# Modulation loads queued behind the written stores, and three fills written before the recurrence's preparation

## The chip, the cores and the metric

The kernel runs on one core of one Trainium2 chip. The metric is the device time of one execution in microseconds (us); lower is better. PE is the matrix engine, DVE the vector engine, ACT the scalar engine, POOL GpSimd and SP the sync engine. SP, ACT and POOL also issue transfers, each in the order of its own instruction stream.

## The reference, cut to what matters

The reference is two layers over 512 latent tokens of width 1024 with 256 context tokens. Each layer starts with a modulation: `silu(c) @ mod_w[i] + mod_b[i]` gives a shift, a scale and a gate.

```python
shift, scale, gate = jnp.split(s_lat @ mod_w[i] + mod_b[i], 3, axis=-1)
h = rms_norm(x, g_pre[i]) * (1.0 + scale[:, None]) + shift[:, None]
...
r, k, v, za, bg, cg, xb, zb = jnp.split(h @ w_in, EVEN_SPLITS, axis=-1)
ya, _, _ = rwkv_seq(rwkv_prep(h, r, k, v, *rw), S_f, S_b, r_k, lnx_w, lnx_b, True)
yb = bg * dwconv(cg * xb, sc_w, seg_len)
y = jnp.concatenate([ya * silu(za), yb * silu(zb)], axis=-1) @ w_out
```

The even layer projects the tokens to r, k, v and five more streams of width 1024. It runs a recurrence over the context in both directions, and then over the latents from the context's last states (`S_f`, `S_b`). The odd layer is a convolution module. The modulation matrix of both layers is 1024 x 3072.

## The kernel before, in words

**Pairs and projections.** The 16 heads are handled as 8 pairs of 128 channels. A projection is one 1024 x 128 column block of the weights. Its matmuls are done three times over 8 row blocks (a high part and a low part of each operand, without low by low), 24 matmuls into one PSUM bank. `project(p, which, rc, between)` does r, k or v (which = 0, 1, 2) of pair p: a context projection (named `pck`, `pcv`) if `rc` is given, then a call of `between`, then a latent projection (`plr`, `plk`, `plv`). The ACT and two DVE instructions of `shifted` (L437, L438, L440) mix neighbouring tokens into the result (`kc`, `vc`, `lk`, `lv`, `lr`) and so empty the bank. The latent result is stored to memory (`psp`) from POOL, L458. `gate(p, 24, "za")` is a projection `pza` with ACT (L874) and DVE (L875), stored from POOL too. k0 stands below for k of pair 0, za4 for the gate of pair 4.

**Weights.** `load_w` brings a block in two halves of 256 KB by SP into two raw buffers (`wrk`, `wrv`, ...). ACT casts each half (L129, `whk`, ...) and DVE subtracts (L130, `wlk`, ...); three buffers each hold the high and the low halves. SP can issue the next half when the subtraction has freed a raw buffer.

**Banks.** Projections alternate between two PSUM banks (`mm0`, `mm1`), so a projection waits until the result before the last one has been emptied. The recurrence's preparation uses the two banks of the tag `at`.

**The modulation in groups.** What the second part of the modulation needs is computed in 16 groups of 1 MB, four transfers of 256 KB and four matmul pairs each, called group 0 to group 15 here. `rest()` is called 17 times between other work. Call n computes group n - 1 and starts the loads of group n + 1. Even groups go to one set of buffers (`mwbtanhl`, `mwbxal`, from group 8 on `ectx`), odd groups to another (`mwr`). Groups 0 and 1 are loaded by SP (L974), the others by POOL (L976). Calls 0 to 3 follow k0, k1, v0 and v1 in `prep_ctx(0, rest)`; calls 4 to 7 stand in `lora` after its row blocks 1, 3, 5 and 7; the others follow in the preparation of pairs 2 and 3.

**The recurrence.** Context stages s = 0 to 3 take two pairs each (`chain_ctx`), latent stages s = 4 to 11 one pair each (`chain_lat`). While stage s runs, the stage after the next is prepared: `light` builds factors on DVE and ACT, `heavy` multiplies them, `solve` inverts a triangle (a chain of small DVE instructions L739 and L741), `merge` puts halves together. Within `heavy`, `pa` is four groups of matmuls (`pal`); each uses both `at` banks, and DVE empties them into `E` (L682). Fills are projections that only later stages need: `fills(x)` writes those that `FILL_R` and `FILL_Z` list under x. `fills(3)` is r3, za4, za5, za6, za7.

**What sets the order.** A scheduler lays out each engine's instruction stream at build time from the dependencies; among what is ready it takes first what was written first, except that the weights' casts go ahead as high priority. The engines then run these streams in order. `tc.issue_after(x)` puts what its block writes on x's engine behind x in that engine's stream, without a wait for x's end. The letters of a stage give the order in which the work is written; the middle entry is used for s = 2 and 3.

```python
STAGE = ("KLSMVHvF", "OPLSMHF", "OSPLMHFC")
...
for gi, (z, g) in enumerate(PA_ORDER if lat else ((0, 0), (1, 0))):
    with anchored(an, ha[gi if lat else 2 * gi]):
```

L is light, S solve, M merge, H heavy, F fills. After stage 3 the convolution branch of pair 0 (`conv_branch(0)`: `pcg`, `pxb`, `pbg`, `pzb`) is written, and then the latent stages.

Of the kernel before, what the change touches and what calls it, by code (L numbers as in the profile page):

```python
# [31 lines left out]
CONV_AFTER = (0, 2, 7, 6)  # L32
PA_ORDER = ((0, 1), (1, 0), (1, 1), (0, 0))
HEAVY = ("ANB", "ANBV")
STAGE = ("KLSMVHvF", "OPLSMHF", "OSPLMHFC")
FILL_R = (0, 0, 2, 3, 4, 4, 4, 4)
FILL_Z = (0, 1, 1, 1, 3, 3, 3, 3)
ZR = (slice(0, 64), slice(64, 128))
# [13 lines left out]
def kernel(ctx: ExitStack, tc: tile.TileContext, I: dict, out: bass.AP):  # L52
# [325 lines left out]
    def lora(hp, w1, between):  # L378
        pwl, pal = (ps.tile([P, 512], F32, tag="zo", name=n, bufs=2) for n in ("pwl", "pal"))
        pwc = ps_at("pwc")  # L380
        for kt in range(KT):
            h1 = hp[kt][:, 1:771]
            dh = w("AR", f"dh{kt}")[:, 0:770]
            V.tensor_tensor(out=dh, in0=hp[kt][:, 0:770], in1=hp[kt][:, 2:772], op=ALU.add)
            for (zi, pl) in ((0, pwl), (1, pal)):
                xw = E1[:, (2 * kt + zi) % 4 * D : (2 * kt + zi) % 4 * D + 770]
                S.activation(xw, h1, AF.Copy, scale=owa[:, zi * 8 + kt : zi * 8 + kt + 1])
                V.scalar_tensor_tensor(out=xw, in0=dh, scalar=hwa[:, zi * 8 + kt : zi * 8 + kt + 1], in1=xw,
                                       op0=ALU.mult, op1=ALU.add)
                lhs = w1[zi][kt // 4][:, kt % 4].rearrange("p a b -> p (a b)")  # L390
                mm(pl, lhs, xw[:, 258:770], kt == 0, kt == KT - 1)
                mm(pwc[:, zi * CTX : (zi + 1) * CTX], lhs, xw[:, 0:CTX], kt == 0 and zi == 0, kt == KT - 1 and zi == 1)
            if kt % 2:
                between()
        lorl.extend([cvp.tile([P, SEQ], F32R, tag=f"{t}{z}", name=f"{t}{z}") for z in range(2)] for t in ("tanhl", "xal"))
        S.activation(lorc[0], pwc[:, 0:CTX], AF.Tanh)
        S.copy(lorc[1], pwc[:, CTX : 2 * CTX])
        for i, pl in enumerate((pwl, pal)):
            t, th = w("tmp", f"lor{i}"), w("tmp", f"lorh{i}", F32R)
            S.activation(t, pl, AF.Copy if i else AF.Tanh)  # L400
            S.copy(th, t)
            for z in range(2):
                rows, hr, lr = (slice(64 * x, 64 * x + 64) for x in (z, i, 1 - i))
                S.copy(lorl[i][z][hr], th[rows])
                V.tensor_tensor(out=lorl[i][z][lr], in0=t[rows], in1=th[rows], op=ALU.subtract)
# [37 lines left out]
    def project(p, which, rc=None, between=None):  # L443
        nm = "rkv"[which] + str(p)
        wt = first_w.pop(nm) if nm in first_w else load_w(which * 8 + p, nm)
        if rc is not None:
            pc = (ps_at if nm in ("k0", "k1") else ps_mm)("pc" + nm)[:, :CTX]
            proj(wt, pc, (hch, hcl))
            shifted(pc, rc, p, which)
            if between:  # L450
                between()
        pl = ps_mm("pl" + nm)
        proj(wt, pl, hlat)
        flip["at"] ^= 1
        tag = ("cg", "yb")[flip["at"]]
        rl = cvp.tile([P, SEQ], F32, tag=tag, name="l" + nm)
        shifted(pl, rl, p, which)
        nc.gpsimd.dma_start(psp[p, which], rl)  # L458

    def state(lat, x):  # L460
        ps_ = [x] if lat else [2 * x, 2 * x + 1]
# [4 lines left out]
    def prep_ctx(b, between=None, st=None, kinds=(1, 2), inner=None, js=(0, 1)):  # L466
        st = st or state(False, b)
        for which in kinds:
            nm = "rkv"[which]
            if nm not in st:  # L470
                st[nm] = w("r_" if which == 1 and b % 2 else nm + "_", nm + st["nm"])
            for p, cs in [st["parts"][j] for j in js]:
                project(p, which, st[nm][:, cs], inner)
                if between:
                    between()
        return st
# [185 lines left out]
    def heavy(st, an=None):  # L662
        ha = (None,) * 4 if an is None else HEAVY_AFTER[an["lat"]]
        lat, nm = st["lat"], st["nm"]
        UV = buf("UV", st)
        E = buf("E", st)
        st["UV"], st["E"], st["BKt"] = UV, E, [buf("BKt", st, z) for z in range(2)]

        def pa():
            for gi, (z, g) in enumerate(PA_ORDER if lat else ((0, 0), (1, 0))):  # L670
                with anchored(an, ha[gi if lat else 2 * gi]):
                    AR, BK = st["AR"][z], st["BK"][z]
                    m, x = (4, P) if lat else (8, CH)
                    c0 = m * g
                    pas = [ch3(ps_at(f"pa{nm}{z}{g}{h}"), x) for h in range(2)]
                    go = pinned(st["ev"] if lat else ())
                    st["ev"] = []
                    for c in range(m):
                        for h in (1, 0):
                            go(pas[h][:, c, :], kb(BK, h, c0 + c), AR[ZR[h], c0 + c, 0:x])  # L680
                    for h in range(2):
                        st["ev"].append(V.tensor_tensor(  # L682
                            out=E[:, h, z * NLAT + c0 : z * NLAT + c0 + m, :], in0=pas[h],
                            in1=maskE[:, z * (1 + h) : z * (1 + h) + 1, 0:x].to_broadcast([P, m, x]), op=ALU.mult))

        def pb():
            for z in range(2):
                pbs = [ch3(ps_at(f"pb{nm}{z}{h}")) for h in range(2)]
                go = pinned(st["ev"] if lat else ())
                st["ev"] = []  # L690
                for c in range(NLAT):
                    for h in (1, 0):
                        go(pbs[h][:, c, :], kb(st["BK"][z], h, c), ident[ZR[h], ZR[h]], op=tr)
                for h in range(2):
                    st["ev"].append(S.copy(st["BKt"][z][:, :, ZR[h]], pbs[h]))

        def nt():
            for h in range(2):
                for b in range(2):
                    rs = slice(64 * (1 - h) + 32 * b, 64 * (1 - h) + 32 * b + 32)  # L700
                    S.copy(Nt[rs], E[rs, h, :, 32 * b : 32 * b + 32])

        def pv():
            pv, v_ = ch3(ps_at(f"pv{nm}")), st["v"]
            for c in range(NLAT):
                for h in range(2):
                    mm(pv[ZR[h], c, :], v_[ZR[h], c * CH : (c + 1) * CH], ctr[ZR[h], ZR[h]], True, True)
            for z in range(2):
                for h in range(2):
                    src = pv[ZR[h]].rearrange("p (j c) x -> p j c x", j=2)  # L710
                    dst = UV[ZR[h], z * NLAT : (z + 1) * NLAT, ZR[h]].rearrange("p (j c) x -> p j c x", j=2)
                    S.copy(dst, src if lat or not z else src[:, :, ::-1, :])

        def po():
            if lat:
                bon = st["bon"]
                pb = ps_at("pbon" + nm)
                mm(pb, blk, bon, True, True)
                V.scalar_tensor_tensor(out=bon, in0=pb, scalar=0.5, in1=st["v"], op0=ALU.mult, op1=ALU.mult)

        st["po"], st["pv"] = po, pv
        for x in HEAVY[lat]:
            {"A": pa, "B": pb, "N": nt, "V": pv, "O": po}[x]()
# [181 lines left out]
    def after(anchor):  # L905
        return tc.issue_after(anchor) if anchor is not None else nullcontext()
# [43 lines left out]
    def rest():  # L950
# [16 lines left out]
        for g in ((n + 1,) if n else (0, 1)):  # L967
            for q in ((0, 1, 2, 3), (3, 2, 1, 0))[g % 2] if g < 16 else ():
                u = 4 * (g // 8) + q
                layer, c0 = (0, 2 * D + 512 * u) if u < 2 else (1, 512 * (u - 2))  # L970
                src = I["mod_w"][layer, g % 8 * P : (g % 8 + 1) * P, c0 : c0 + 512]
                if g < 2:
                    with tc.issue_after(env["last"].ins):
                        nc.sync.dma_start(home(g, q), src)  # L974
                else:
                    nc.gpsimd.dma_start(home(g, q), src)  # L976

    def rested(half_, acc):
        row = w("HP", f"mrow{half_}")
# [10 lines left out]
        if half_ == 0:  # L990
            V.memset(acc, 0.0)

    def fills(x):
        for p in range(8):
            if FILL_R[p] == x:
                project(p, 0)
            if FILL_Z[p] == x:
                gz = gate(p, 24, "za")
                nc.gpsimd.dma_start(psp[p, 3], gz)

    sts = [prep_ctx(0, rest)]
    whs, behind = first_w["spectra"]
    with tc.issue_after(behind):
        for ns, wh in whs:
# [19 lines left out]
    for s in range(12):  # L1024
# [11 lines left out]
        for x in STAGE[(s >= 2) + (s >= 4)]:  # L1036
# [16 lines left out]
                light(sts[s + 2], st)  # L1053
            elif x == "H" and s < 10:
                heavy(sts[s + 2], st)
            elif x == "F":
                fills(s + 1)
                if s >= 4:
                    finish(st)
            elif x == "C":  # L1060
# [383 lines left out]
```

## Time and profile before

| | |
|---|---|
| median of 3 runs | 1385.95 us (1385.75 to 1392.3) |
| the profiled execution | 1392.7 us |
| its span, first to last instruction | 1390.9 us |
| busy: PE, DVE, ACT, POOL | 1337.1, 985.3, 745.3, 127.4 us |
| mean granted clock of PE | 0.992 |

A timeline row gives start and duration in us, the engine, the line, the operation, out<-in, and in brackets the engine's idle time before it and what ended that. A window row gives start and end, the length, the busy time and count of each engine (PE, weight loads, DVE, ACT, POOL), PE's granted clock (1 is full speed), the busy share of the DMA engines and GB/s.

### The profile page before, as it was taken

The numbers are of one execution on the slowest core, as the hardware profiler recorded it, in microseconds if no ns is written. First come the engines' busy times: TensorE is split into PE (matmuls) and PEld (weight loads), VectorE is DVE, ScalarE is ACT, GpSimd is POOL, SyncE is SP. The second block draws the span as 40 slices with busy tenths as digits, with TensorE's granted clock in tenths as the row PEclk, the third lists the DMA queues.
The fourth block names the chain that finished last, engine by engine and source line by source line (L and its number), as shares of the span: only waits on it lengthen the run. The fifth ranks groups of instructions, "written<-read, shape, count | busy, mean of one in ns | idle before, by whom it ended". The sixth has DMA issues, their size and how long they took to land.

```text
span 1390.9 us, 29758 instructions
## 1 busy us (share of the span) xinstructions
PE 1337.1 (96%) x11925; PEld 995.2 (72%) x11925; DVE 985.3 (71%) x2304; ACT 745.3 (54%) x1509; POOL 127.4 (9%) x263
## 2 busy tenths in 40 slices
PE   6989999999899999999999999999999999999998
PEld 2646777777677766676666676677777787788886
DVE  5846879868999599989999998557654653644323
ACT  6536366546756566665666755547742432554222
POOL 4123200001111010101101000010000000000000
PEclk9999999999999999999999999999999999999999
DMA  9855521222323312223222221578621322133232
GB/s 333 254 190 190 189 77 57 87 79 86 88 90 101 99 63 79 70 65 88 82 73 70 76 70 57 183 238 290 222 62 61 121 64 58 61 112 101 91 103 79
DMA packets 139756, 158.55 MB, mean 114 GB/s; under 512 B 15504, under 2 KB 104224, under 8 KB 139498
## 3 DMA queue, kind: packets, MB, share of 16 engines
q1 hardware_dynamic: 123152, 106.47, 24.7%
q0 software_dynamic: 15856, 49.12, 10.8%
q8 instruction: 94, 1.54, 0.5%
q10 hardware_dynamic: 608, 1.06, 0.2%
q14 instruction: 46, 0.37, 0.1%
HBM read 138.33 MB, written 18.28 MB: 113 GB/s over the span
## 4 chain that ended last, share of the span: by engine, by line
PE 66%; DVE 16%; ACT 6%; issue 6%; DMA 5%; SPq 0%; POOL 0%; DVEq 0%; ACTq 0%; POOLq 0%
PE pu L57 10%; PE pz L57 6%; PE f L57 6%; PE uh L57 4%; PE zol L57 4%; PE pcg L57 4%; PE o L57 4%; PE plk L57 3%; PE pxb L57 3%; PE plr L57 2%; PE plv L57 2%; PE pzb L57 2%; DVE E L682 2%; PE pck L57 1%; PE zoc L57 1%
## 5 line engine op out<-in xcount | busy, mean ns | idle before, releaser
L57 PE MATMUL o<-wh,y 128*128 128x512 f32 x248 | 79.7, 397 | 0.0
L739 DVE TENSOR_TENSOR xtmpl<-Xl,Yl 128x126 f32<-128x126 f32 (+22 forms) x248 | 61.9, 250 | 2.8
L741 DVE TENSOR_TENSOR Yl<-Yl,xtmpl 128x126 f32<-128x126 f32 (+22 forms) x248 | 61.9, 250 | 2.7
L1257 ACT CAST ah<-a 64x512 fp32r<-64x512 f32 x32 | 19.8, 618 | 72.6 <-DVE a L1252 72.2
L57 PE MATMUL zol<-UV,E 64*64 64x64 f32 (+1 forms) x1024 | 54.0, 221 | 0.0
L57 PEld LDWEIGHTS o<-wh,y 128*128 128x128 f32 x248 | 45.9, 188 | 9.5
L57 PE MATMUL o<-wl,y 128*128 128x512 f32 x124 | 49.6, 400 | 2.0 <-DVE wl L130 2.0
L57 PE MATMUL pal<-ARl,BKl 64*128 64x128 f32 x512 | 45.7, 298 | 5.8 <-DVE E L682 5.2
L57 PE MATMUL zol<-Hl,ARl 64*64 64x64 f32 x896 | 50.2, 230 | 0.7 <-DVE Hl L854 0.4
L847 ACT COPY UV<-uh 64x128 f32<-64x128 f32 x128 | 33.3, 260 | 32.5 <-PE uh L57 25.0
L57 PEld LDWEIGHTS zol<-Hl,ARl 64*64 64x64 f32 x896 | 34.9, 133 | 20.0 <-issue 15.1
L130 DVE TENSOR_TENSOR wl<-wr,wh 128x1024 fp32r<-128x1024 f32 x28 | 34.2, 1223 | 20.6 <-ACT wh L129 20.5
L57 PEld LDWEIGHTS pal<-ARl,BKl 64*128 64x128 f32 x512 | 36.1, 193 | 16.9 <-issue 10.2
L57 PEld LDWEIGHTS uh<-UV,BKt 128*64 128x64 f32 x704 | 26.3, 137 | 30.3 <-ACT UV L847 23.4
L1252 DVE TENSOR_TENSOR a<-pu,a 128x512 f32<-128x512 f32 x16 | 11.0, 690 | 47.7 <-PE pu L57 45.4
L57 PEld LDWEIGHTS zol<-UV,E 64*64 64x64 f32 (+1 forms) x1024 | 42.2, 136 | 2.8 <-ACT UV L847 2.1
L682 DVE TENSOR_TENSOR E<-pal,maskE 128x512 f32<-128x512 f32 x64 | 43.0, 682 | 0.5 <-PE pal L57 0.3
L1209 DVE SCALAR_TENSOR_TENSOR pr<-px,dbe,What 119x512 f32<-119x512 f32 x32 | 22.6, 747 | 26.6 <-PE px L57 26.6
L129 ACT CAST wh<-wr 128x1024 fp32r<-128x1024 f32 x28 | 29.6, 1057 | 21.3 <-PE o L57 10.7
L854 DVE SCALAR_TENSOR_TENSOR Hl<-uh,PCl,HPl 128x64 f32<-128x64 f32 x112 | 26.4, 277 | 19.4 <-PE uh L57 9.2
L57 PE MATMUL uh<-UV,BKt 128*64 128x64 f32 x704 | 36.3, 232 | 3.3 <-ACT UV L847 2.0
L57 PEld LDWEIGHTS uh<-Ol,E 64*64 64x64 f32 x512 | 19.9, 133 | 24.5 <-ACT Ol L841 17.3
(996 smaller groups left out, 4206.1 us busy)
## 6 DMA issues: line engine op xcount, KB each, us to landing
wr<-in_ev_w_out_dram SPq DMA_DIRECT2D x28, 512.0 KB, 5.2
mwr<-in_mod_w_dram POOLq DMA_DIRECT2D x28, 256.0 KB, 4.3
wrv<-in_ev_w_in_dram SPq DMA_DIRECT2D x16, 256.0 KB, 3.1
ectx<-in_mod_w_dram POOLq DMA_DIRECT2D x16, 256.0 KB, 4.2
wrr<-in_ev_w_in_dram SPq DMA_DIRECT2D x16, 256.0 KB, 2.9
wrza<-in_ev_w_in_dram SPq DMA_DIRECT2D x16, 256.0 KB, 2.8
wrcg<-in_ev_w_in_dram SPq DMA_DIRECT2D x16, 256.0 KB, 2.8
wrxb<-in_ev_w_in_dram SPq DMA_DIRECT2D x16, 256.0 KB, 3.0
```

The costliest lines, as they stand in the source:

```text
L57: env["pe"] = T.matmul(o, lhsT, rhs, start=start, stop=stop)
L129: S.copy(hi, raw)
L130: env["lo"].tensor_tensor(out=lo, in0=raw, in1=hi, op=ALU.subtract)
L682: st["ev"].append(V.tensor_tensor(out=E[:, h, z * NLAT + c0 : z * NLAT + c0 + m, :], in0=pas[h], in1=maskE[:, z * (1 + h) : z * (1 + h) + ...
L739: V.tensor_tensor(out=tv, in0=X[:, :i, i : i + 1].to_broadcast([P, i, m]), in1=Y[:, i : i + 1, c0:].to_broadcast([P, i, m]), op=ALU.mult)
L741: V.tensor_tensor(out=Y[:, :i, c0:], in0=Y[:, :i, c0:], in1=tv, op=ALU.add)
L847: u_ = S.copy(UV[ZR[1 - h], i : 2 * nch - i : 2 * nch - 1 - 2 * i, ZR[h]], uh[ZR[1 - h], 0:2, :])
L854: h_ = V.scalar_tensor_tensor(out=Hn[:, z, :], in0=uh[:, 2 + z, :], scalar=PC[z][:, i : i + 1], in1=HP[:, z, :], op0=ALU.mult, op1=ALU.add)
L1209: V.scalar_tensor_tensor(out=pr[s][:NPROD], in0=px[s][:NPROD], scalar=dbe[:, 0:1], in1=What[:, n * 512 : n * 512 + 512], op0=ALU.add, op1= ...
L1252: V.tensor_tensor(out=a, in0=pp[1], in1=a, op=ALU.mult)
L1257: S.copy(ahl[s][hr], a[hr])
```

## The change

There are two parts.

1. The POOL loads of a modulation group are put behind the last store of a latent r, k or v result that was written before them (`env["store"]`), in POOL's stream. One call of `rest()` is moved: it leaves `lora`'s row block 1 and stands inside v1, between its context and its latent projection. So group 2 is computed and group 4's load written inside v1 (before: after v1), group 3 is computed and group 5's load written after v1 (before: in `lora`'s row block 1); from call 5 on the calls stand where they stood.
2. In stage s = 2 three of the five fills (r3, za4, za5) are written ahead of `heavy` (letter f), the other two (za6, za7) after it as before. The last matmul of za5 is kept as `hold`, and the groups 1 to 3 of `pa` in that `heavy` are put behind it in PE's stream. Stage 3 has the letter too, but does nothing there.

```diff
-STAGE = ("KLSMVHvF", "OPLSMHF", "OSPLMHFC")
+STAGE = ("KLSMVHvF", "OPLSMfHF", "OSPLMHFC")
...
-            if kt % 2:
+            if kt % 2 and kt > 1:
                 between()
...
-        nc.gpsimd.dma_start(psp[p, which], rl)
+        env["store"] = nc.gpsimd.dma_start(psp[p, which], rl)
...
-                project(p, which, st[nm][:, cs], inner)
+                project(p, which, st[nm][:, cs], inner if b or (p, which) == (1, 2) else None)
...
-                with anchored(an, ha[gi if lat else 2 * gi]):
+                with anchored(an, ha[gi if lat else 2 * gi]), after(st.get("hold") if gi else None):
...
-                    nc.gpsimd.dma_start(home(g, q), src)
+                    with tc.issue_after(env["store"].ins):
+                        nc.gpsimd.dma_start(home(g, q), src)
...
-    def fills(x):
-        for p in range(8):
-            if FILL_R[p] == x:
+    def fills(x, first=0, last=None):
+        for kind, p in [(kind, p) for p in range(8) for kind in "RZ" if (FILL_R, FILL_Z)[kind == "Z"][p] == x][first:last]:
+            if kind == "R":
                 project(p, 0)
-            if FILL_Z[p] == x:
+            else:
...
-    sts = [prep_ctx(0, rest)]
+    sts = [prep_ctx(0, rest, inner=rest)]
...
+            elif x == "f" and s == 2:
+                fills(s + 1, 0, 3)
+                sts[s + 2]["hold"] = env["pe"].ins
             elif x == "F":
-                fills(s + 1)
+                fills(s + 1, 3 if s == 2 else 0)
```

## The prediction

> **What bounds the kernel now.** I read the page's busy shares and chain first, then the matrix engine's timeline for its idle times, and for each large one the timelines of the engines it waited for.
>
> ```profile
> PE 1337.1 (96%) x11925; PEld 995.2 (72%) x11925; DVE 985.3 (71%) x2304; ACT 745.3 (54%) x1509; POOL 127.4 (9%) x263
> PE 66%; DVE 16%; ACT 6%; issue 6%; DMA 5%; SPq 0%; POOL 0%; DVEq 0%; ACTq 0%; POOLq 0%
> ```
>
> PE is busy 1337.1 of 1390.9 us, so 53.8 us of idle time are all that reordering can win, and the change alters no arithmetic. The two largest idle times of PE after the first 10 us are these, each in a place that the change touches.
>
> ```profile
> 72.24 1.04 PE L57 MATMUL uh<-mwr,s 128*2 128x512 f32 x8
> 74.30 0.48 PE L57 MATMUL pcv<-hctx,whv 128*128 128x256 f32 x2 [1.02 <-DVE vc L440]
> 80.94 0.76 PE L57 MATMUL plv<-hlh,whv 128*128 128x512 f32 x1 [3.56 <-DVE lv L440]
> 88.86 1.04 PE L57 MATMUL uh<-mwr,s 128*2 128x512 f32 x8
> ...
> 376.87 0.68 PE L57 MATMUL zoc<-UV,ectx 64*64 64x64 f32 x16
> 381.45 2.08 PE L57 MATMUL pal<-ARl,BKl 64*128 64x128 f32 x16 [3.90 <-DVE E L682]
> ```
>
> They cost more than their length, for PE runs at half clock behind each:
>
> ```profile
> 77.30:81.00 3.70, 0.14 (x2) 0.09 (x1) 2.30 (x4) 1.57 (x3) 0.00 (x0) 0.94 0.79 261
> 81.00:84.00 3.00, 3.00 (x7) 2.39 (x8) 0.68 (x2) 0.00 (x0) 0.55 (x1) 0.50 0.49 160
> ...
> 381.50:388.00 6.50, 6.50 (x37) 5.14 (x39) 6.19 (x19) 0.00 (x0) 1.10 (x2) 0.52 0.21 81
> ```
>
> 3.00 us at 0.50 lose 1.5 us of work; 6.50 us at 0.52 lose 3.1.
>
> **Part 1, the loads behind the stores.** It adds and removes no instruction; on POOL it moves groups of four load issues past a store, and one call of `rest()` (8 matmul rows, 1.04 us by the row at 72.24, and four load issues) from behind v1 into v1. Why does v1 wait? The rows of ACT, DVE, POOL and SP:
>
> ```profile
> 72.42 0.62 ACT L129 CAST whv<-wrv 128x512 fp32r<-128x512 f32 x1 [5.06 <-DMA wrv<-in_ev_w_in_dram]
> 78.01 0.62 ACT L129 CAST whk<-wrk 128x512 fp32r<-128x512 f32 x1 [4.11 <-DMA wrk<-in_ev_w_in_dram]
> 78.53 0.68 ACT L437 ACTIVATE lv<-plv,omu 128x512 f32<-128x512 f32 x1
> 73.07 0.69 DVE L130 TENSOR_TENSOR wlv<-wrv,whv 128x512 fp32r<-128x512 f32 x1 [4.72 <-ACT whv L129]
> 80.05 0.75 DVE L440 SCALAR_TENSOR_TENSOR lv<-plv,hmu,lv 128x511 f32<-128x511 f32 x1
> 62.04 1.09 POOL L976 DMA_DIRECT2D mwbtanhl<-in_mod_w_dram  x2 [12.44 <-PE uh L57]
> 65.11 0.55 POOL L458 DMA_DIRECT2D psp<-lk  x1 [0.38 <-ACT ectx L387]
> 73.56 2.13 POOL L976 DMA_DIRECT2D mwr<-in_mod_w_dram  x4 [7.90 <-PE uh L57]
> 81.34 0.55 POOL L458 DMA_DIRECT2D psp<-lv  x1 [5.65 <-issue]
> 63.93 1.63 SPq L126 DMA_DIRECT2D wrv<-in_ev_w_in_dram  x2
> 73.79 13.11 SPq L126 DMA_DIRECT2D wrk<-in_ev_w_in_dram  x4
> DMA to landing us min/median/max: 8.0/8.2/8.5
> wrv<-in_ev_w_in_dram SPq DMA_DIRECT2D x16, 256.0 KB, 3.1
> ```
>
> The first of the last two rows is from the tile view of `wrv`, 63 to 66 us. v1's two weight halves, issued at 63.93 and 65.19, took 8.0 and 8.5 us; the median of that kind is 3.1. Around them run group 2's 1 MB (from 62.04) and two stores. So v1's first cast is at 72.42 instead of about 67, its subtraction at 73.07 holds up `vc` behind it on DVE (the gap of 1.02), and it frees the raw buffer for k2's half only at 73.76, so SP issues that at 73.79, next to group 3's 1 MB (73.56 to 75.69). ACT stands in front of k2's cast until 78.01, and v0's shift is queued behind that cast: `lv` on ACT at 78.53, on DVE to 80.80. v1's latent projection wants that bank: 3.56 us.
>
> After the change group 2's loads follow k1's store (about 64.7), 65.2 to 67.3, and group 3's follow v0's store. The first half of v1 lands about 63.93 + 3.1 = 67.0; the second, issued with group 2, I put at 70. DVE does `vc` before 73.28, when group 1's matmuls end: −1.02. k2's half is issued near 69 and meets no group 3; 5 us for it give 74. Its cast ends near 74.6, then `lv` takes 0.68 on ACT and 2 x 0.75 on DVE: 76.8. On PE v1's context part runs 73.28 to 76.36 (its 3.08 us now), then come group 2's matmuls, 1.04 us: 77.40. The bank is free by then: −3.56, and with the idle time the half clock behind it, −1.5.
>
> What is late next: group 3 is now wanted after v1, at 77.40 + 24 x 0.23 = 82.9.
>
> ```profile
> 363.35 0.39 PE L57 MATMUL plr<-hlh,wlr 128*128 128x512 f32 x1
> 363.58 0.39 PE L57 MATMUL pza<-hlh,whza 128*128 128x512 f32 x1
> DMA to landing us min/median/max: 3.6/4.6/4.8
> 125.00 1.06 POOL L976 DMA_DIRECT2D ectx<-in_mod_w_dram  x2 [8.48 <-PE mpb L57]
> 129.88 0.55 POOL L458 DMA_DIRECT2D psp<-lk  x1 [2.25 <-ACT iPc L599]
> 136.65 1.04 PE L57 MATMUL mpb<-ectx,s 128*2 128x512 f32 x8
> DMA to landing us min/median/max: 3.0/3.9/4.4
> ```
>
> (0.23 is the step from row to row at 363; the landing rows are of `mwr`, 73 to 76, and `ectx`, 124 to 128.) v0's store goes out at 76.8, four issues of 0.53 follow, the last at 78.9, and 4.8 make 83.7: PE may wait up to 0.8; I take +0.6. Group 4's loads, behind these, were at 89.32 before and come earlier. The same order later: group 10's loads stood at 125.00, ahead of k2's store at 129.88; behind it the last is issued at 132.0 and lands at 136.4, and its matmuls are at 136.65. So +0.2 here, between 0 and the 5.4 us by which the loads move. Groups 12 and 14 lose one to three issue slots of 0.5 with longer covers; nothing. Nobody waits long for the stores themselves; they now leave earlier.
>
> Part 1: −1.02 − 3.56 − 1.5 + 0.6 + 0.2 = −5.3 us, with ends at −6.1 (no wait for groups) and −1 (the halves no faster).
>
> The Trainium skill, page "DMA: Bandwidth & Descriptors", section "Queues, rings and completion order", says that each DMA engine takes turns between its queues packet by packet. By that rule POOL's megabyte could at most double a weight half's 3.1 us, to 6.2, whether it is issued 2 us before or 2 us behind; v1's first half would have landed at 70.1. The trace has it later (8.5 us), so waiting behind the megabyte is real here; by the rule alone part 1 would come to about −4 us, since group 2's load still runs beside v1's second half.
>
> **Part 2, the fills before the preparation.** The number of matmuls stays. On PE za4's last two go ahead of `pa`'s first group, and za5 (24 x 0.23 = 5.5 us) ahead of groups 1 to 3. On ACT and DVE the shift of r3 and the gates of za4 and za5 go ahead of the emptying of `E`, on POOL their stores with them; SP brings their weights as before. PE's idle time ends when za5 can start, and za5 wants r3's bank.
>
> ```profile
> 370.39 0.68 ACT L437 ACTIVATE lr<-plr,omu 128x512 f32<-128x512 f32 x1
> ...
> 379.01 0.68 DVE L632 TENSOR_TENSOR BKl<-kdl,iPl 128x512 f32<-128x512 f32 x1
> 379.61 0.29 DVE L739 TENSOR_TENSOR xtmpc<-Xc,Yc 128x130 f32<-128x130 f32 x1
> 379.82 0.68 DVE L682 TENSOR_TENSOR E<-pal,maskE 128x512 f32<-128x512 f32 x1
> 380.62 0.68 DVE L682 TENSOR_TENSOR E<-pal,maskE 128x512 f32<-128x512 f32 x1
> 381.41 0.74 DVE L438 SCALAR_TENSOR_TENSOR lr<-plr,hmu,lr 128x511 f32<-128x511 f32 x1
> 382.26 0.74 DVE L440 SCALAR_TENSOR_TENSOR lr<-plr,hmu,lr 128x511 f32<-128x511 f32 x1
> ```
>
> r3's matmuls end at 363.6 and ACT's part at 371.07, but DVE comes to it at 381.41, behind `light` (L632 is its last) and the two instructions on `E`. Written before `heavy`, r3's shift takes the two slots of `E`, 379.82 and 380.62, and ends at 381.4; it stays behind `light`, which is written before it. So za5 starts at 381.4, where `pal` starts now: 0 won. Ends: −7.0 if DVE reaches r3 before 377.5 (3.90 + 3.1), +3 if `pa`'s groups, 8 us later, leave PE waiting for `E` twice (two emptyings of 1.5 us each). I take 0, since the rows of DVE show no free slot before 379.6.
>
> What queues behind the hold is `E`, then `solve` and `merge` of pair 0 and the latent recurrence. That has cover:
>
> ```profile
> 470.00:480.00 10.00, 10.00 (x46) 8.29 (x45) 4.87 (x7) 3.13 (x5) 0.00 (x0) 1.00 0.28 81
> 482.41 0.45 PE L57 MATMUL zol<-h,ARl 64*64 64x64 f32 x8
> ```
>
> Up to 482.41 PE is full with the convolution branch, while DVE is half idle; a preparation 8 us late still fits there.
>
> **Sum.** −5.3 + 0 on the profiled execution's 1392.7 (span 1390.9): 1387.4. The profiled one is 6.75 us above the median of the three runs, whose own highest is 1392.3; I carry the difference over: 1385.95 − 5.3 = 1380.6 us.
>
> **Rivals.**
> - *Both idle times go.* The build may find r3's shift a slot inside `light` (DVE waits 0.2 to 0.3 us there now and then), and za5 then fills PE from 377.5. Against it stands DVE's solid row of work up to 379.6. −5.3 − 7.0: 1373.6.
> - *Nothing comes of it.* k2's cast stays in front of `lv` on ACT and its half still takes 4 to 5 us next to group 2; the bank stays late and only contention with group 3 goes, some 1 us: 1385. For it: ACT's order there is fixed by the build; against it, 8 us of landing are out of line.
> - *The loads come late, and it gets slower.* A load behind a store waits for the shift before that store, and shifts of latent projections starve behind `light`: r3's waited from 363.6 to 383.0, 19.4 us. If k2's did so (its last matmul is at 123.7), its store would leave at 143.1, group 10 land at 143.7 + 1.6 + 4.4 = 149.7, and PE, in order, wait 13 us: 1380.6 + 13 = 1393.6. It decides from a store later than 130 on; it outweighs the gain from 135.4 on. Against it: the row at 129.88 is only 6 us behind those matmuls.
>
> **How the numbers follow.** A change of 0.5%, 6.9 us, is about what a measurement here can tell from none: faster is below 1379.0, slower above 1392.9. Forecast 0.42, with a range of its own from 1376 to 1385, so 0.16 faster and 0.26 same. Both go 0.25, nearly all faster (0.24). Nothing comes of it 0.23, same. Late loads 0.10, 0.08 of it slower. That makes 0.40, 0.52 and 0.08. The range runs from 1372 (both go, a little over) to 1388 (nothing, plus a new wait of 2 us); it leaves out the late loads and the tails.
>
> The Trainium skill, page "TensorE: Matmul & The Clock Gate", section "What's actually happening", has the clock halve after an idle window of about 3.4 us and return after a busy one of the same length. By it the 0.52 over 6.50 us would have been 3.4 us long behind 381.45, and a dense za5 in that place would win some 1.6 us more than my 0; the trace shows two windows there.
>
> **What will show it.** Right: no idle time over 0.5 us before v1's `plv`, group 2's matmuls between `pcv` and `plv`, the tile view of `wrv` below 6 us, clock 1.00 there; `lr` on DVE ahead of `E`, near 3.9 us of idle time before za5. Wrong: a wait of PE on a group's DMA over 1 us, `lr` before 377, or new idle times of PE between 390 and 480.

## The result: 0.6% slower

| | before | after |
|---|---|---|
| median | 1386.92 us (1384.35 to 1395.52, 14 runs) | 1396.74 us (1393.35 to 1402.54, 14 runs) |
| ratio after / before | | 1.0063, 95% interval 1.0047 to 1.0078 |
| profiled execution, span | 1392.7, 1390.9 us | 1395.22, 1393.1 us |

Forecast were 1380.6 us and a range of 1372 to 1388. The change made the kernel slower by some 9 us.

The busy shares, from the page of the profile after:

```profile
PE 1338.1 (96%) x11925; PEld 993.5 (71%) x11925; DVE 987.7 (71%) x2304; ACT 744.2 (53%) x1509; POOL 127.9 (9%) x263
```

The work is the same. PE's busy time grew by 1.0 us and the span by 2.2 only, because the profiled execution of before was a slow one for that kernel; after's is a typical one for after. These two traces alone therefore mislead about the size. They do show where to look. The early part: rows of PE's timeline, the landing row of the tile view of `wrv` (60 to 67 us), and a window row, in which PE's clock is the third figure from the end:

```profile
75.83 0.28 PE L57 MATMUL pcv<-hctx,wlv 128*128 128x256 f32 x1
76.04 0.60 PE L57 MATMUL uh<-mwbtanhl,s 128*2 128x512 f32 x2
82.83 2.20 PE L57 MATMUL uh<-mwr,s 128*2 128x512 f32 x8
130.54 1.84 PE L57 MATMUL mpb<-ectx,s 128*2 128x512 f32 x8
160.84 2.13 PE L57 MATMUL mpb<-ectx,s 128*2 128x512 f32 x8
...
DMA to landing us min/median/max: 2.9/3.4/3.9
...
80.00:90.00 10.00, 10.00 (x36) 5.27 (x35) 4.84 (x6) 4.50 (x6) 5.04 (x10) 1.00 0.92 315
```

Both idle times of v1 are gone, group 2's matmuls stand between `pcv` and `plv`, the weight halves land after 2.9 and 3.9 us instead of 8.0 and 8.5, and the clock is 1.00. But look at the durations: eight matmuls of a modulation group, 1.04 us before, now take 2.20 (group 3), 1.84 (group 10) and 2.13 (group 12). PE waits inside these rows for parts of their loads, which now stand behind a store. No idle time is printed, and the window calls PE 100% busy.

The third stage and what follows, first three rows of PE in the kernel before, then PE and DVE after:

```profile
442.66 1.16 PE L57 MATMUL pal<-ARl,BKl 64*128 64x128 f32 x16
452.85 1.20 PE L57 MATMUL uh<-aml,E 32*32 32x32 f32 x64 [0.55 <-DVE aml L748]
458.22 0.40 PE L57 MATMUL pcg<-hlh,whcg 128*128 128x512 f32 x1
...
377.28 0.78 PE L57 MATMUL pza<-hlh,whza 128*128 128x512 f32 x1 [3.84 <-DVE lr L440]
384.55 1.16 PE L57 MATMUL pal<-ARl,BKl 64*128 64x128 f32 x16
436.95 1.16 PE L57 MATMUL pal<-ARl,BKl 64*128 64x128 f32 x16 [2.25 <-DVE E L682]
438.59 0.66 PE L57 MATMUL plr<-hlh,whr 128*128 128x512 f32 x1 [0.47 <-DVE lr L440]
452.14 0.71 PE L657 MATMUL pbl<-ident,BKl 64*128 64x64 f32 x16 [0.76 <-ACT BKt L695]
459.00 1.20 PE L57 MATMUL uh<-aml,E 32*32 32x32 f32 x64 [1.46 <-DVE aml L748]
460.71 0.40 PE L57 MATMUL pcg<-hlh,whcg 128*128 128x512 f32 x1
521.00 1.16 PE L57 MATMUL pal<-ARl,BKl 64*128 64x128 f32 x16 [1.67 <-DVE E L682]
524.37 2.08 PE L57 MATMUL pal<-ARl,BKl 64*128 64x128 f32 x16 [2.21 <-DVE E L682]
...
393.48 0.69 DVE L766 COPY ectx<-uh 32x512 f32<-32x512 f32 x1 [1.19 <-ACT ectx L766]
396.86 1.29 DVE L682 TENSOR_TENSOR E<-pal,maskE 128x512 f32<-128x512 f32 x2 [1.39 <-PE pal L57]
400.63 2.04 DVE L733 STREAM_TRANSPOSE Xl<-Nt 128x1024 f32<-128x1024 f32 x1 [1.71 <-ACT Nt L701]
```

za5 starts where the forecast had it, behind r3's shift and 3.84 us of idle time. Then `pa`'s groups 1 to 3 come late, DVE stands idle three times for over 1 us (there was none over 0.5 in that place), `solve` of pair 0 begins with the 2.04 us row at 400.63, and PE waits four times between 430 and 460 us and twice near 520. The row at 436.95 is the second of `pa`'s groups for pair 1; in the kernel before it is the row at 442.66, and PE doesn't wait there.

### The profile page after: what moved, and what is told of

Its sections match the earlier page's. It is cut to its first block, busy times and chain, and to the rows that moved or that the text cites. A ratio compares the mean times of both kernels' runs of the same rounds, so it can differ in the third digit from the quotient of the medians.

```text
span 1393.1 us, 29762 instructions
## 1 busy us (share of the span) xinstructions
PE 1338.1 (96%) x11925; PEld 993.5 (71%) x11925; DVE 987.7 (71%) x2304; ACT 744.2 (53%) x1509; POOL 127.9 (9%) x263
## 4 chain that ended last, share of the span: by engine, by line
PE 66%; DVE 14%; ACT 7%; issue 5%; DMA 3%; POOL 0%; DVEq 0%; SPq 0%; ACTq 0%; POOLq 0%
PE pu L57 10%; PE pz L57 6%; PE f L57 6%; PE uh L57 4%; PE o L57 4%; PE zol L57 4%; PE pcg L57 4%; PE pxb L57 3%; PE plv L57 3%; PE plk L57 2%; PE plr L57 2%; PE pzb L57 2%; DVE E L682 2%; PE pcv L57 1%; PE pck L57 1%
```

## Three stretches

Three stretches between starts of PE's rows serve as a ruler below, since they don't depend on what an execution lost earlier. **S1** runs from v0's first `pcv` matmul (62.91 us before) to the first `zoc<-UV,ectx` of stage 0 (196.94); **S2** from the `zoc<-UV,ectx` at 357.8 to pair 1's first `pcg` (486.15); **S3** from there to pair 2's first `pcg` (544.14). All in us, one profiled execution each; the ratio is that of 6 to 14 runs to the kernel before, with its 95% interval.

| kernel | S1 | S2 | S3 | ratio |
|---|---|---|---|---|
| before | 134.0 | 128.4 | 58.0 | |
| before_again | 130.2 | 127.9 | 58.0 | |
| after | 129.8 | 132.9 | 62.1 | 1.0063 (1.0047 to 1.0078) |
| p1_alone | 130.1 | 128.4 | 58.0 | 1.0001 (0.9984 to 1.0018) |
| p2_alone | 130.8 | 133.9 | 63.3 | 1.0083 (1.0064 to 1.0101) |
| r3_before_heavy | 130.4 | 129.0 | 58.0 | 1.0014 (0.9999 to 1.0029) |
| fills2 | 130.8 | 129.3 | 58.0 | 1.0014 (0.9993 to 1.0035) |
| r3_first | 129.8 | 126.7 | 58.0 | 0.9993 (0.9979 to 1.0007) |
| early_only | 128.8 | 128.4 | 58.0 | 1.0004 (0.9985 to 1.0023) |
| early_nomove | 128.8 | 128.4 | 58.0 | 0.9997 (0.9978 to 1.0017) |
| dve_pad | 130.2 | 129.0 | 58.0 | 1.0009 (0.9989 to 1.0029) |
| after_pad | 130.1 | 133.0 | 62.2 | 1.0076 (1.0058 to 1.0094) |
| after_conv | 129.1 | 130.1 | 57.4 | 1.0017 (0.9999 to 1.0035) |
| p1_conv | 131.2 | 130.8 | 59.4 | 1.0027 (1.0012 to 1.0041) |
| after_bgw | 131.5 | 133.6 | 58.0 | 1.0048 (1.0033 to 1.0063) |
| best | 129.6 | 126.9 | 58.0 | 0.9995 (0.9980 to 1.0010) |

Against p1_alone the change costs 4.5 us in S2 and 4.1 in S3, 8.6 together; its ratio is 0.62% above that of p1_alone, 8.6 us too. So these two stretches hold the loss. In both it is idle time of PE: in S2 11.5 us against 7.3 in p1_alone, nearly all of it in the waits between 429 and 460 us (5.5 against 1.3); in S3 the 1.67 and 2.21 us near 520.

How well do the stretches repeat? Ten kernels have part 1 unaltered and so the same program in S1: 129.1 to 131.5. The program before gave 134.0, 130.2 and 130.8 (p2_alone has it up to the third stage). S2 is 127.9 to 128.4 in the five executions that leave the third stage alone, and S3 is 58.0 wherever its order stayed. So a difference of 1 us in S1 or of half a microsecond in S2 is no finding. Outside the three stretches it is no better: from the end of S3 to the end of the span, before and before_again, one program, took 846.8 and 842.9 us.

## The experiments

### The two parts one by one

**p1_alone**: part 1 without part 2.

```diff
-STAGE = ("KLSMVHvF", "OPLSMfHF", "OSPLMHFC")
+STAGE = ("KLSMVHvF", "OPLSMHF", "OSPLMHFC")
...
-with anchored(an, ha[...]), after(st.get("hold") if gi else None):
+with anchored(an, ha[...]):
...
-                fills(s + 1, 3 if s == 2 else 0)
+                fills(s + 1)
```

> Part 1 without part 2: the loads behind the stores and the moved call of rest(), the fills where they were. Theory A (part 1 wins, part 2 loses): the gaps of 1.02 and 3.56 us and the half clock behind them are gone, PE is 4 to 6 us ahead of before from 100 us to the end of the third stage and stays so: ratio 0.9955 to 0.997 (1380.5 to 1382.5 against 1386.9). Rival B (the early gain is given back later whatever the fills do, as later transfers and recurrences set their own pace): ratio 0.998 to 1.001. Rival C (part 1 itself causes the later losses, by the moved loads): ratio 1.002 to 1.007.

**p2_alone**: part 2 without part 1.

```diff
-            if kt % 2 and kt > 1:
+            if kt % 2:
...
-project(p, which, st[nm][:, cs], inner if b or (p, which) == (1, 2) else None)
+project(p, which, st[nm][:, cs], inner)
...
-                    with tc.issue_after(env["store"].ins):
-                        nc.gpsimd.dma_start(home(g, q), src)
+                    nc.gpsimd.dma_start(home(g, q), src)
...
-    sts = [prep_ctx(0, rest, inner=rest)]
+    sts = [prep_ctx(0, rest)]
```

> Part 2 without part 1: r3, za4, za5 ahead of the preparation with the hold, loads and rest() as before. Theory A (part 2 costs what the change lost): PE waits for DVE between 430 and 460 us and again at about 520 us, and the end is 11 to 16 us later: ratio 1.008 to 1.012. Rival B (part 2 costs the 8 or 9 us of the change by itself, part 1 gives nothing at the end): ratio 1.005 to 1.007. Rival C (part 2 costs nothing, as forecast): ratio 0.998 to 1.002.

Theory A held for part 2 and fell for part 1. p2_alone: 1399.96 against 1387.62 us. p1_alone: 1387.27 against 1387.62, rival B's number, although its trace has none of the idle times. Up to the third stage p2_alone is the program before. PE's rows, first of p2_alone, then of p1_alone:

```profile
72.86 0.47 PE L57 MATMUL pcv<-hctx,whv 128*128 128x256 f32 x2 [0.60 <-DVE vc L440]
78.54 0.47 PE L57 MATMUL plv<-hlh,whv 128*128 128x512 f32 x1 [2.60 <-DVE lv L440]
85.02 1.04 PE L57 MATMUL uh<-mwr,s 128*2 128x512 f32 x8
132.37 1.04 PE L57 MATMUL mpb<-ectx,s 128*2 128x512 f32 x8
161.93 1.04 PE L57 MATMUL mpb<-ectx,s 128*2 128x512 f32 x8
```

```profile
83.03 1.26 PE L57 MATMUL uh<-mwr,s 128*2 128x512 f32 x6
84.45 1.02 PE L57 MATMUL uh<-mwr,s 128*2 128x512 f32 x2 [0.15 <-DMA mwr<-in_mod_w_dram]
85.40 1.12 PE L57 MATMUL pwl<-ectx,w 128*128 128x512 f32 x2
130.99 2.23 PE L57 MATMUL mpb<-ectx,s 128*2 128x512 f32 x8
161.69 2.02 PE L57 MATMUL mpb<-ectx,s 128*2 128x512 f32 x8
```

Without part 1 PE loses 0.60 + 2.60 = 3.2 us ahead of v1's projections. With it, group 3 takes 2.37 us (83.03 to 85.40) instead of 0.97 (the step from 85.02 to the next row), and groups 10 and 12 take 1.19 and 0.98 more: 3.6 us. One is paid with the other, and S1 is 130.1 against 130.8, a difference that it shows without any edit too.

**before_again**: the kernel before, profiled once more.

> The kernel before, profiled once more. Theory F (the idle times ahead of v1's two projections belong to the program, their length to the execution): a wait before pcv and one before plv at 73 to 81 us again, together 2.5 to 4.6 us, weight halves of v1 landing after 7 us or more, no clock at half behind them for sure. Rival H (the 4.6 us were of that one execution): less than 1 us in the two places together.

```profile
77.27 0.47 PE L57 MATMUL plv<-hlh,whv 128*128 128x512 f32 x1 [2.36 <-DVE lv L440]
...
DMA to landing us min/median/max: 7.0/7.2/7.5
...
80.00:84.00 4.00, 4.00 (x26) 2.44 (x28) 1.25 (x2) 1.82 (x3) 0.00 (x0) 1.00 0.28 84
```

2.36 us, just below theory F's range; the late weight halves (7.0 to 7.5 us) are there again, the half clock is not. The idle times belong to the program, but 4.58 us and the 1.5 behind them were the bad end of three executions: 4.58, 3.20, 2.36. S1 of the profiled execution of before is 3.8 and 3.3 us above that of the other two.

### Keeping part 1's gain

**early_only** and **early_nomove**: part 1 alone, with only groups 2 and 3 behind a store; early_nomove also leaves the call of `rest()` where it was (the lines of p2_alone above).

```diff
-                    with tc.issue_after(env["store"].ins):
+                    with (tc.issue_after(env["store"].ins) if g < 4 else nullcontext()):
```

> Part 1 alone, but only the loads of groups 2 and 3 go behind a store; the later ones are issued where they were before. Theory F (part 1 wins its 3 to 4.6 us of idle time before v1's plv and gives 3.6 back as waits of PE inside the matmul rows of groups 3, 10 and 12, 1.4 + 1.2 + 1.0): the rows of groups 10 and 12 (near 131 and 162 us) are back at 0.97 us from 2.2 and 2.0, that of group 3 stays near 2.4, and PE is 2.2 us further ahead at 170 us than with all of part 1: ratio 0.997 to 0.999. Rival B (the time before 170 us does not reach the end): ratio 0.9995 to 1.001 with the same rows.

> As early_only, but the call of rest() stays in lora's row block 1, so that group 3 is wanted 2.5 us or more later. Theory F: the wait in group 3's row goes as well (0.97 us), both idle times of v1 stay away because group 2's loads still go behind k1's store: PE 3 to 4.5 us ahead of before at 170 us, ratio 0.9965 to 0.9985. Rival G (it is the moved call, group 2's matmuls between v1's two projections, that covers the late bank, not the order of the loads): an idle time of 1 to 2.6 us before plv comes back, ratio 0.999 to 1.001.

Rows of group 3 and group 10 in early_only, then of `plv` and group 3 in early_nomove:

```profile
84.07 2.54 PE L57 MATMUL uh<-mwr,s 128*2 128x512 f32 x8
132.11 1.04 PE L57 MATMUL mpb<-ectx,s 128*2 128x512 f32 x8
```

```profile
75.21 0.47 PE L57 MATMUL plv<-hlh,whv 128*128 128x512 f32 x1 [0.52 <-ACT vc L437]
81.70 2.03 PE L57 MATMUL uh<-mwr,s 128*2 128x512 f32 x8
```

Group 10 no longer waits, as theory F of these two runs says (it is another than before_again's). Group 3 waits even where its matmuls are behind the unmoved call (2.03, not 0.97), which F had not expected; and the idle time ahead of `plv` stays at 0.5 us without the moved call, so rival G fell: it is the order of the loads that clears v1. S1 is 128.8 in both, 1.4 us below p1_alone and 1.4 to 2 below the two usual executions of before. The runs show no difference (1.0004 and 0.9997): rival B's numbers, though 1.5 us lie inside the intervals of some 0.2% on each side. In these two executions the stretch between S1 and S2 is longer than in p1_alone, 162.8 and 163.2 us against 161.3, and takes the 1.4 us back; best, with early_nomove's order up to there, has 161.2, so this belongs to the executions and is as large as the gain that was looked for.

### How many fills

**r3_before_heavy** and **fills2**: part 1 with one (r3) or two (r3, za4) fills ahead of `heavy`, no hold.

```diff
-                fills(s + 1, 0, 3)
-                sts[s + 2]["hold"] = env["pe"].ins
+                fills(s + 1, 0, 1)        # fills2: 0, 2
...
-                fills(s + 1, 3 if s == 2 else 0)
+                fills(s + 1, 1 if s == 2 else 0)        # fills2: 2
```

> Part 1, and of part 2 only r3 ahead of heavy; za4 and za5 behind it as in the kernel before, no hold. Theory A (what costs is the 8 us of za4 and za5 on PE ahead of pa's groups 1 to 3, which leaves DVE without work): pa's groups follow each other as before, DVE has no idle times over 1 us between 386 and 406, and the ratio is 0.995 to 0.999. Rival D (what costs is r3's shift ahead of E on DVE): ratio 1.003 to 1.008, with solve beginning as late as in the changed kernel. Rival E (any change of the written order in this stage makes the build lay out all later stages anew, and the loss is a matter of that layout): a loss or gain that begins behind 460 us, with no new idle time of DVE at 386 to 406.

> Part 1, and r3 and za4 ahead of heavy, za5 behind it as before, no hold. Between r3 alone (1.0014) and the whole change (1.0063). Theory A (the loss is the time by which the fills keep pa's groups, and so DVE, waiting): za4 stood almost wholly ahead of pa's second group already, so little is added: 1.000 to 1.003, DVE without work for at most 2 us between 386 and 406, solve of pair 0 begins within 4 us of its place in part 1 alone. Rival E (a new layout of all later stages makes the loss, whatever the fills do in this one): anything from 0.998 to 1.007, and no relation to DVE's idle time at 386 to 406.

In S2 r3 costs 0.6 us and r3 with za4 1.0, both hardly more than S2 varies by itself; all three cost 4.5, and S3 is lost only with all three. za5 is the expensive one. r3_before_heavy doesn't quite meet theory A: DVE has one idle time of 1.21 us there, and the ratio is above 0.999. The hold itself does nothing: the instruction streams that the build makes of the change without it are the same on every engine.

**r3_first**: part 1, and r3 written ahead of `light` instead.

```diff
-STAGE = ("KLSMVHvF", "OPLSMfHF", "OSPLMHFC")
+STAGE = ("KLSMVHvF", "OPfLSMHF", "OSPLMHFC")
```

(with the lines of r3_before_heavy)

> Part 1, and r3 alone written ahead of light, the rest of the fills where they were. Theory A: r3's shift is no longer behind light on DVE, so its bank is free before 377 and za4 and za5 can run without the 3.9 us of idle time while DVE builds; DVE ends light 2.2 us later (0.68 + 2 x 0.74), pa's groups keep their order: ratio 0.993 to 0.998. Rival D (DVE is the pacing engine up to 460 us, and 1.5 us put ahead of light come back as a wait of PE later): ratio 0.997 to 1.003. Rival E (a new layout of all later stages): a difference of either sign that begins behind 460 us.

The idle time shrinks from 3.90 to 2.62 us and S2 to 126.7, but the ratio is 0.9993: rival D's range holds it, theory A's not.

### Is a late preparation covered?

**dve_pad**: part 1 alone, with ten sums over `E` added on DVE, so that `solve` of pair 0 is late.

```diff
                 heavy(sts[s + 2], st)
+                if s == 2:
+                    gpad = wk.tile([P, 32], F32, tag="orq", name="gpad")[:, 0:4]
+                    for _ in range(10):
+                        V.tensor_reduce(gpad, sts[4]["E"][:, 0, 0:4, :].bitcast(F32), mybir.AxisListType.X, ALU.add)
```

> Part 1 alone with ten extra instructions on DVE (sums over E, 128x512 each, into a scratch column that nothing reads), written behind heavy in stage s = 2, so that they delay solve of pair 0 by 5 to 7 us and leave PE's fills and pa's groups alone. Theory A (DVE sets the pace from 346 to 460 us and its time there is not covered): PE waits for uh<-aml and pal near 440 to 460 us and the end is 4 to 8 us later than part 1 alone: ratio 1.003 to 1.006. The prediction's step (a preparation 8 us late still fits, since the convolution branch covers it up to 482 us): ratio 0.999 to 1.001.

The group of the added instructions, and PE's rows behind it (the last matmul of `pcg` ahead of `uh<-aml`, and that):

```profile
L1060 DVE TENSOR_REDUCE gpad<-E 128x4 f32<-128x512 f32 x10 | 6.8, 679 | 0.1
...
457.82 0.40 PE L57 MATMUL pcg<-hlh,wlcg 128*128 128x512 f32 x1
459.54 1.20 PE L57 MATMUL uh<-aml,E 32*32 32x32 f32 x64 [1.32 <-DVE aml L748]
```

6.8 us of DVE work cost 0.7 us in S2, and 1.0009 against 1.0001 can't be told apart. Theory A, that DVE's time up to 460 us is the path, fell here. The prediction's step held here: a late preparation is covered. It is as late as in the changed kernel: `uh<-aml` starts 104.8 us behind the start of S2, in the changed kernel 105.0, in p1_alone 95.1. So lateness alone is not what costs 4.5 us. What differs is what PE's stream has ahead of the late work. 18 matmuls of `pcg` stand ahead of `uh<-aml`; in the kernel before all of them stood behind it (458.22 behind 452.85), where nothing was late, and in the changed kernel they still do (460.71 behind 459.00). And between the first and the second of `pa`'s groups for pair 1 stand 36 matmuls of r fills, in p1_alone 35, in the changed kernel only 16; there PE waits 2.25 us for `E` (436.95), in the other two not at all. So a new theory, P: the cover is there, but PE takes its stream in order, and in the changed kernel the cover stands behind the late work.

**after_pad**: the same ten sums in the changed kernel.

> The changed kernel with the ten extra DVE sums over E written behind heavy in stage s = 2 (some 7 us of work on DVE whose result nothing reads). The build knows of them and puts 30 matmuls of the convolution branch (pcg, pxb) ahead of merge's uh<-aml in PE's stream; in the changed kernel these stand behind it. Theory P (the preparation that comes late has enough cover, but PE takes its stream in order and the changed kernel's order has the cover behind the late work): more work on DVE, and yet the same time or a better one than the changed kernel: ratio 1.001 to 1.006, the wait before uh<-aml near 459 us under 0.5. Theory A (DVE's time up to 460 us is the path): another 5 to 7 us, ratio 1.010 to 1.012.

```profile
435.54 2.08 PE L57 MATMUL pal<-ARl,BKl 64*128 64x128 f32 x16 [2.50 <-DVE E L682]
465.07 1.20 PE L57 MATMUL uh<-aml,E 32*32 32x32 f32 x64 [1.45 <-DVE aml L748]
```

S2 is 133.0 against 132.9: 6.8 us more work on DVE for nothing, against theory A's 5 to 7. Theory P's other numbers were missed: `uh<-aml` still waits 1.45 us, though all 24 matmuls of `pcg` now stand ahead of it, and 1.0076 is above its range and below A's (the intervals of 1.0076 and 1.0063 overlap). So where `pcg` stands against `uh<-aml` is not what costs the 4.5 us. The other place has not changed: 15 matmuls of r fills between `pa`'s first and second group, and a wait of 2.50 us behind them.

**after_conv**: the changed kernel with `conv_branch(0)` written ahead of r4 to r7. **p1_conv**: the same on part 1 alone.

```diff
             elif x == "F":
+                if s == 3:
+                    G.memset(cx[:, :, 0:66:65], 0.0)
+                    conv_branch(0)
                 fills(s + 1, 3 if s == 2 else 0)
...
         if s == 3:
-            G.memset(cx[:, :, 0:66:65], 0.0)
-            conv_branch(0)
```

> The changed kernel with the convolution branch of pair 0 written ahead of the fills of stage 3 (r4 to r7) instead of behind them. In PE's stream pcg, pxb, pbg, pzb then stand between pa's groups of the next pair (410 to 455 us) and r4 to r7 behind merge. Theory P: the waits of 2.25, 0.47, 0.76 and 1.46 us between 430 and 460 us mostly go, since convolution fills need a smaller share of DVE than r fills (whose two shifts of 0.74 us hold the banks): 4 to 7 us won against the changed kernel, ratio 0.999 to 1.003. Theory A: DVE is late all the same and PE waits as before: ratio 1.005 to 1.008. The idle time of 3.9 us in stage 5's preparation (521 and 524 us) shows apart from this whether it belongs to the order there.

> Part 1 alone, with the convolution branch of pair 0 written ahead of r4 to r7. A try for a faster kernel: with part 1 alone PE waits only 0.5 to 0.6 us at a time between 400 and 460 us (0.46, 0.32, 0.52), so theory P gives at most 1 to 2 us: ratio 0.997 to 1.001. If order in this stretch is worth more than these waits: below 0.996.

```profile
440.60 1.16 PE L57 MATMUL pal<-ARl,BKl 64*128 64x128 f32 x16 [0.15 <-DVE E L682]
455.50 1.20 PE L57 MATMUL uh<-aml,E 32*32 32x32 f32 x64 [1.08 <-DVE aml L748]
390.00:400.00 10.00, 10.00 (x159) 7.78 (x152) 6.07 (x10) 3.94 (x7) 0.00 (x0) 1.00 0.16 52
```

DVE's hole behind za5 is still there (6.07 of 10 us busy, the third busy time of the window row), and yet the waits for `E` and for r's shift are gone or short: 27 matmuls of the convolution branch stand between `pa`'s first and second group, and PE has no idle time there. S2 falls by 2.8 us, S3 by 4.7, the ratio to 1.0017. Theory P's range. On part 1 alone, where there was no late work to cover, the same edit costs 2.5 us in S2 and the ratio is 1.0027, above what was expected: the order isn't better as such. Taken as a pair the two are the clearest result: in this order part 2 costs nothing (S2 130.1 with it, 130.8 without it), in the old one 4.5 us. One thing stays open: a convolution projection's bank isn't emptied by r's two shifts on DVE, and in the changed kernel the next r fill waited for that shift too (0.47 us, 438.59). Whether it is the place of the cover or its kind, no run here separates.

### The second loss

**after_bgw**: the changed kernel, with high priority for the casts of one weight block.

```diff
-        with tc.high_priority() if env["first"] else nullcontext():
+        with tc.high_priority() if env["first"] or name[:-1] == "bg1" else nullcontext():
```

> The changed kernel, with one thing more: the casts and subtractions of one weight block of the convolution branch of pair 1 (bg1) are given high priority, as those of the first four stages have it. In the changed kernel both of its low halves are made by DVE only at 524.5 and 525.3 us, behind the emptying of E, so that pbg's matmuls stand behind pa's last groups and PE waits 1.67 and 2.21 us for E at 521 and 524 us with half a clock behind them. Theory P (order, not work): pbg stands between pa's groups again, both waits go, and the time is 3 to 6 us below the changed kernel's: ratio 1.002 to 1.0045. Rival A (DVE is late in this stage from the one before, and PE waits for it in whatever order): the waits move to E or to aml behind pbg, ratio 1.0055 to 1.007.

The changed kernel has these rows near 520 us (PE's, around the two waits shown above, and the clock behind them, 0.50):

```profile
518.17 1.16 PE L57 MATMUL pal<-ARl,BKl 64*128 64x128 f32 x16
526.38 0.79 PE L57 MATMUL pbg<-hlh,wlbg 128*128 128x512 f32 x1
524.10:527.50 3.40, 3.13 (x19) 2.71 (x20) 3.07 (x11) 0.30 (x1) 0.00 (x0) 0.50 0.29 84
L130 DVE TENSOR_TENSOR wlbg<-wrbg,whbg x2: 679/680/681, 524.5 to 525.3; 128x512 fp32r<-128x512 f32 x2
```

and after_bgw has these:

```profile
529.94 0.50 PE L57 MATMUL pbg<-hlh,wlbg 128*128 128x512 f32 x1
534.94 1.16 PE L57 MATMUL pal<-ARl,BKl 64*128 64x128 f32 x16 [0.21 <-DVE E L682]
L130 DVE TENSOR_TENSOR wlbg<-wrbg,whbg x2: 692/692/693, 513.8 to 523.4; 128x512 fp32r<-128x512 f32 x2
```

In the changed kernel `pbg`'s third matmul needs `wlbg`, which DVE makes at 524.5, behind the emptyings of `E`; so nothing stands between `pa`'s groups, and PE waits 1.67 and 2.21 us. With `wlbg` started at 513.8, in an execution that is 8.9 us later at the start of S3, `pbg` fills these places, and S3 is 58.0 again: 4.1 us won by the order of two small instructions. Theory P for the place. The ratio, 1.0048, falls by 0.15% only, half of what S3 shows and just outside P's range; its interval reaches down to 1.0033. The profiled execution, 1401.33 us, is the slowest of its ten; the 8.9 us lie ahead of S3, in places where PE's stream is the changed kernel's. What made the build put these two instructions later in the changed kernel is open.

**best**: early_nomove with r3_first's fill.

> Against the kernel before: only the loads of groups 2 and 3 go behind a store, no moved call, and r3 is written ahead of light. Neither half of this showed a difference alone (0.9997 and 0.9993). If their gains in the traces are real and add up (1.5 us of the early stage against a usual run of the kernel before, and 1.5 to 2.7 us in the third stage): ratio 0.997 to 0.9985. If not: 0.999 to 1.001.

S1 and S2 together are 2 us below p1_alone, the ratio is 0.9995. No version here beats the kernel before by more than the runs can tell.

## Why the prediction was wrong, step by step

- **Part 1, the idle times (−1.02 − 3.56 − 1.5).** The mechanism was right: 8 us landings, the casts behind them, the late bank; all of it is gone, and group 2 stands where it was forecast. The size was off: it was read from one execution, 6.75 us above the median, and then subtracted from the median. Two other executions of the same program lose 3.20 and 2.36 us there without a half clock. Part of the 6.75 us that the forecast carried over was the very loss that it then took off again: S1 of that execution is 3.3 to 3.8 us above the other two.
- **Part 1, what is late next (+0.6 + 0.2, nothing for groups 12 and 14).** Group 3 +1.16, group 10 +0.80, group 12 +1.09 in the changed kernel (2.20, 1.84, 2.13 against 1.04). The rule that was used, last issue plus landing, was right for group 3 in kind; the "longer covers" of group 12 were an assertion without a row. One of the prediction's own signs of being wrong, a wait of PE on a group's DMA over 1 us, is met by groups 3 and 12. Together part 1 is worth 0.0 ± 0.2% instead of −5.3 us.
- **The rule on queues that take turns by packet** (the Trainium skill, "DMA: Bandwidth & Descriptors", section "Queues, rings and completion order") was said to give at most 6.2 us for a half. The three executions of the old order show 7.0 to 8.5 us for halves issued 2 us behind the start of a group's megabyte; the changed kernel, where they go out ahead of it, shows 2.9 and 3.9. So the trace stands against that bound. It doesn't stand against the rule: "at most double" took the packets of both queues as equal, and in the trace of before, 62 to 74 us, they are not (packets, MB, share of the engines; `q0` is POOL's queue, `q1` SP's):

```profile
q0 software_dynamic: 480, 1.57, 47.2%
q1 hardware_dynamic: 1286, 0.62, 17.7%
```

That is 3.3 KB a packet against 0.5. If the two queues take turns packet by packet, POOL's moves some seven times as many bytes in the meantime (an estimate from these two rows), and a half can wait for most of the megabyte. No run here varies the packets, so that this is the whole of it is not shown. The −4 us for part 1 by the bound was no better than my −5.3.
- **Part 2, where za5 starts: 0.** Right: r3's shift ahead of `E` on DVE, 3.84 us of idle time ahead of za5.
- **Part 2, what queues behind it: "a preparation 8 us late still fits there".** This is the step that failed. The preparation is as late as was forecast: `solve` begins 46.7 us behind the start of S2, in p1_alone 38.6. But the cover was read from a window at 470 to 480 us, and PE comes to the late work before it comes there: it waits at 437, 452 and 459 us, 4.5 us in S2. dve_pad shows that a preparation whose `uh<-aml` is just as late costs 0.7 us where more matmuls stand ahead of these places in PE's stream. after_conv put other matmuls there and won 2.8 of the 4.5 us back. The prediction did not ask whether PE's order reaches the cover before the late work.
- **Not in the sum at all:** that a change of the written order makes the build lay out all that follows anew. The other 4.1 us (S3) arose 140 us behind the edit. The end of +3 for part 2, PE waiting for `E` twice, had the right kind of wait (437, 521 and 524 us), but it was left at an end, and it was too small by a factor of three.
- **The rivals.** The slower one was looked for in late loads at k2: its store left in time (123.77), and group 10 cost 0.80 us and not 13. Its sign was right, its place wrong. "Nothing comes of it" had part 1's number by another way: the waits went, and others came. The named sign of error, "new idle times of PE between 390 and 480", is what came.
- **The clock rule** (the Trainium skill, "TensorE: Matmul & The Clock Gate", section "What's actually happening"): a dense za5 behind the gap was to have one half-clock window instead of two. The trace of the changed kernel agrees:

```profile
379.99 0.63 PE L57 MATMUL pza<-hlh,whza 128*128 128x512 f32 x1
380.42 0.55 PE L57 MATMUL pza<-hll,whza 128*128 128x512 f32 x1
380.80 0.39 PE L57 MATMUL pza<-hlh,wlza 128*128 128x512 f32 x1
```

From 377.28 the rows step by 0.43 us, from 380.80 by 0.23 again: half clock for some 3.5 us, where before it was 0.52 over 6.50. What that saved was lost again behind the wait at 437, where PE's rows step by 0.43 us once more. On the other half of the rule, an idle window of about 3.4 us, the trace does not agree: the clock was 0.50 from 524.10 to 527.50, and PE's idle times there were 1.67 us (up to 521.00) and 2.21 us (up to 524.37), both shorter; the measurement decides.

## What to carry to other kernels

Cover is a matter of order: an in-order engine has it only if the covering work stands ahead of the waiting work in its own stream, so look up both positions before costing a delay at nothing. A wait read from one execution, above all from one above the median, may be an upper end and not the term; look at the same rows in a second execution. And when a greedy build lays out the streams, an edit of written order is a change of everything behind it, so its range must be that of a new layout.

## What the runs showed of the hardware

- A wait for data can hide inside a busy row: the eight matmuls of a group print 2.20 us instead of 1.04, with no idle time and a window at 10.00 of 10.00 busy. Steps between starts of rows show it.
- The twelve runs of best spread from 1383.54 to 1390.96 us. The granted clock goes with it, though not alone: 0.998 took 1383.97 and 0.990 took 1390.96, but at 0.993 there are both 1387.78 and 1385.64, and 0.994 took 1383.54. Differences of 0.2% need many runs here, whatever a pair of traces says.
